# Sums of squares over partitions for nine RMS norms: ones as the weights in four column groups, in place of ones as the moving column

## The chip, the cores and the metric

The kernel runs on one core of one Trainium2 chip. The metric is the device time of one execution in microseconds (us); of several runs the median is given. The engines are named as in the profile: PE is TensorE's matmul, PEld its weight load, DVE is VectorE, ACT ScalarE, POOL GpSimd, SP the engine that issues most transfers.

## The reference

One layer of a decoder is applied to 1024 prompt tokens and 32 sample tokens, each a vector of 1024 numbers in float32. What matters here is how often a token's vector is normalized:

```python
def _rms(x, g):
    xf = x.astype(jnp.float32)
    y = xf * lax.rsqrt(jnp.mean(xf * xf, axis=-1, keepdims=True) + EPS)
    return (y * g.astype(jnp.float32)).astype(x.dtype)

def _layer(x, p, attn_fn, pool_prev, pos0, ...):
    h = _rms(x, n_mix_pre)
    z = h @ w_in                      # q, k, v and the pooling input
    ...                               # sliding-window attention, pooling mixer
    mix = jnp.concatenate([a, m], axis=-1) @ w_out
    x = x + _rms(mix, n_mix_post)
    f = _rms(x, n_ffn_pre)
    f = (jax.nn.silu(f @ w_gate) * (f @ w_up)) @ w_down
    x = x + _rms(f, n_ffn_post)
    x = x + jax.nn.sigmoid(x @ w_ple_gate) * (p @ w_ple)
    return x, k_state, v_state, pool_state
```

There are four norms per token. Each needs the sum of a token's 1024 squares, and then its reciprocal root as a factor for the whole vector.

## The kernel before

**Layout.** Features lie on the 128 partitions and tokens along the free dimension, so a vector of 1024 features is eight blocks of 128 partitions. The 1056 tokens form three groups, 0, 1 and 2, of 352 tokens each; group 2 holds the end of the prompt and the 32 sample tokens. Four norms for three groups are twelve norms. The three of the first kind come at the kernel's start, the other nine later.

**Matmuls.** Every operand is split into a high part (`wh`, `fh`, ...) that is rounded to a matmul type and the remainder (`wl`, `fl`, ...). A product of two operands is three matmuls: high by high, high by low, low by high (`gemm`). ScalarE makes the high part of a tile with a cast (L173), VectorE the low part with a subtraction (L174). Weights pass through four pairs of such tiles; a cast of new weights can start when TensorE is done with an older pair. A projection of one group onto 128 output features is 24 matmuls with 352 moving columns.

**One norm** is the generator `rstd_steps(acc)`. `acc` is a tile of 128 partitions by 352 tokens that holds partial sums of squares, so a sum over partitions is left to do. Three float32 matmuls take a block of 128 columns of `acc` as weights and one column of ones as what moves; each gives one column of a bank, with tokens on the partitions. ScalarE takes the root into `sd`, a tile of 128 by 3, VectorE its reciprocal, and splits it into a high and a low part (`hl`). Then two VectorE products spread each of the two parts on diagonals (`dg`), the generator pauses with a `yield`, and after it two matmuls with ones as weights turn the diagonals into a bank in which every partition holds the factors of all 352 tokens.

**What sets the order.** On TensorE the matmuls keep the order in which the program records them. Work that runs between projections is written as generators (`chain`). After every product the program calls `turn(n)` with the number of matmuls, which advances a clock, `now`; a generator whose due time has come is resumed there. A pause `yield load, wait` sets the next due time: the load divided by `share` is added to VectorE's planned clock and the wait to that. So the two numbers of a `yield` decide behind which matmuls the next matmul of that generator stands. On the other engines a scheduler sets the order when the program is built, and each engine then works strictly in it.

**Where the nine norms are.** `ffn_steps(g)` holds two for each group, `mix`'s norm and that ahead of the feed-forward part: between the two it scales and adds, squares, and sums (`sum_halves`). After the second it makes the gain products (L982, `y` from `x`, a gain column and the bank with the factors), four to each half of the features, and splits each half into `fh` and `fl`. Group 2's runs beside the last output projections, and its operand is read by the first feed-forward matmuls; those of groups 0 and 1 run beside the feed-forward matmuls of group 2. `x2_steps(g, operand)` holds the third norm of each group, behind the feed-forward part. The other names in the timelines: `mh`, `ml` are the mixed operands of the output projection, `acc<-acc,sq` (L854) adds a square to a sum of squares, `b` is a bank of PSUM.

Of the kernel before, what the change touches and what calls it, by code (L numbers as in the profile page):

```python
# [10 lines left out]
F32 = mybir.dt.float32  # L11
F32R = mybir.dt.float32r
AF = mybir.ActivationFunctionType
ALU = mybir.AluOpType
AX = mybir.AxisListType

P = 128
D = 1024
# [44 lines left out]
def trunk_kernel(  # L63
# [33 lines left out]
    te, ve, se, ge = nc.tensor, nc.vector, nc.scalar, nc.gpsimd  # L97
# [4 lines left out]
    spool = ctx.enter_context(tc.tile_pool(name="spool", bufs=2))  # L102
# [5 lines left out]
    def nm(s):  # L108
        cnt[0] += 1
        return f"{s}{cnt[0]}"  # L110

    def act_tile(shape, dt=F32, s="a"):
        return apool.tile(shape, dt, tag="a", bufs=A_SLOTS, name=nm(s))
# [12 lines left out]
    def mm(*args, **kw):  # L126

        ins = te.matmul(*args, **kw)  # L128
        if pinned[0]:
            tc.keep_in_program_order(ins)  # L130

    def bank():
        return psum.tile([P, 512], F32, tag="b", name=nm("b"))
# [4 lines left out]
    def const(shape, src=None, s="c", dt=F32):  # L138
        t = cpool.tile(shape, dt, name=nm(s))
        if src is not None:  # L140
            nc.scalar.dma_start(t, src)
        return t
# [3 lines left out]
    ident = const([P, P])  # L146
# [8 lines left out]
    ones = const([P, P])  # L155
    ge.memset(ones, 1.0)
    ones_r = const([P, P], dt=F32R)
    ge.tensor_copy(ones_r, ones)
    epst = const([P, 1])
# [7 lines left out]
    def fix(ins):  # L167

        if fixed[0]:
            tc.keep_in_program_order(ins)  # L170

    def split(hi, lo, src):
        fix(se.copy(hi, src))  # L173
        fix(ve.tensor_tensor(lo, src, hi.bitcast(F32), op=ALU.subtract))  # L174
# [177 lines left out]
            for k in range(KC)  # L352
        ]

    def rstd_steps(acc):

        n = acc.shape[1]
        sm = bank()  # L360
        for i in range(TB):
            at = min(i * P, n - P)
            mm(sm[:, i : i + 1], acc[:, at : at + P], ones[:, 0:1], start=True, stop=True)
        sd = spool.tile([P, TB], F32, tag="sd", name=nm("sd"))
        fix(se.activation(sd, sm[:, :TB], AF.Sqrt, bias=epst, scale=1.0 / D))
        fix(ve.reciprocal(sd, sd))
        hl = spool.tile([P, 2, TB], F32R, tag="hl", name=nm("hl"))
        fix(ve.tensor_copy(hl[:, 0], sd))
        fix(ve.tensor_tensor(hl[:, 1], sd, hl[:, 0].bitcast(F32), op=ALU.subtract))
        dgs = []  # L370
        dg2 = act_tile([P, 2, TB, P], F32R, "dg")
        for h in range(2):
            dg = dg2[:, h]
            fix(
                ve.tensor_tensor(
                    dg, diag, hl[:, h].bitcast(F32).unsqueeze(2).to_broadcast([P, TB, P]), op=ALU.mult
                )
            )
            dgs.append(dg.rearrange("p i k -> p (i k)"))
        yield 6, 14  # L380
        ps = bank()
        for h in range(2):
            mm(ps[:, :n], ones_r, dgs[h][:, :n], start=h == 0, stop=h == 1)
        return ps[:, :n]

    def acc_rows():
        t = act_tile([P, 4, NX], s="acc")
        return [t[:, g, : NS[g]] for g in range(G)]
# [30 lines left out]
    xs, acc1, r1 = [[None] * 2 for _ in range(G)], acc_rows(), [None] * G  # L419
# [105 lines left out]
    def u_prod(c, g, h):  # L525

        if h == 0:
            ups[c, g] = bank()
        ps = ups[c, g][:, : NS[g]]
        wh, wl = pairs[U0[c]]  # L530
        xh, xl = xs[g][h]
        for k in range(4):
            mm(ps, wh[:, 4 * h + k, :], xh[:, k, :], start=h == 0 and k == 0, stop=False)
            mm(ps, wh[:, 4 * h + k, :], xl[:, k, :], start=False, stop=False)
        for k in range(4):
            mm(ps, wl[:, 4 * h + k, :], xh[:, k, :], start=False, stop=h == 1 and k == 3)
# [5 lines left out]
    def u_norm(steps, g):  # L542
        try:
            next(steps)
        except StopIteration as e:
            fix(se.copy(acc1[g], e.value))
            r1[g] = acc1[g]

    pinned[0] = True
    norms = [None] * G  # L550
    norms[0] = rstd_steps(acc1[0])
    for h in range(2):
        for c in range(4):
            u_prod(c, 0, h)
# [11 lines left out]
    x_operand(2, 1)  # L566
    for c in range(4):
        u_prod(c, 1, 1)
    norms[1] = rstd_steps(acc1[1])
    u_norm(norms[1], 1)  # L570
    for h in range(2):
        u_prod(0, 2, h)
# [3 lines left out]
    for c in range(4):  # L576
        u_evict(c, 1)
        se.copy(u_decode(c)[:, :, 0:PST], stt[:, c])
    split(wplh, wpll, wpl)
    norms[2] = rstd_steps(acc1[2])  # L580
    u_norm(norms[2], 2)
    for h in range(2):
        u_prod(1, 2, h)
# [131 lines left out]
    def scores(b):  # L715


        t = act_tile([P, 8, WIN])
        nk = 2 * WIN if b else WIN
        lo = b * WIN + WIN - nk  # L720
        at = WIN * 4 // nk
        both = [[bank() for _ in range(4 // at)] for _ in range(2)]
        for c in range(4):
            for kv in range(2):
                rows = slice(64 * kv, 64 * kv + 64)
                i = c % at
                mm(
                    both[kv][c // at][:, i * nk : (i + 1) * nk],
                    qT[c][rows, b * WIN : (b + 1) * WIN],
                    kT[rows, lo : lo + nk],  # L730
                    start=True,
                    stop=True,
                )
        for kv in range(2):
            tk = t[:, 4 * kv : 4 * kv + 4, :]
            for i, ps in enumerate(both[kv]):
                tc_ = tk[:, i * at : (i + 1) * at, :]
                v = ps.rearrange("p (c k) -> p c k", k=nk)
                if b:
                    m = am[:, 0, :].unsqueeze(1).to_broadcast([P, at, WIN])  # L740
                    se.copy(tc_, v[:, :, :WIN])
                    ve.copy_predicated(tc_, m.bitcast(mybir.dt.int32), v[:, :, WIN:])
                else:
                    ve.tensor_tensor(tc_, v, m4(1), op=ALU.add)
            hs = slice(4 * kv, 4 * kv + 4)
            softmax(tk, 4, 0.125, skp[:, hs], nskp[:, hs])
        return t
# [98 lines left out]
    acc = acc_rows()  # L846
# [46 lines left out]
    t = scores(order[0])  # L893
# [16 lines left out]
    for a, b in zip(order, order[1:] + [None]):  # L910
# [11 lines left out]
        t = t2  # L922
# [559 lines left out]
```

## Time and profile before

| What | us |
|---|---|
| median of 3 runs (1087.38 to 1088.51) | 1088.09 |
| the profiled execution's own time | 1088.29 |
| its span, first to last instruction | 1086.5 |
| PE busy in the span | 1076.8 |
| PEld busy | 1060.1 |
| DVE busy | 873.2 |
| ACT busy | 512.4 |
| POOL busy | 283.2 |

A row of a timeline gives the start and the length in us, the engine, the line, the operation, what is written and what is read, the shapes and the number of instructions that the row merges; in brackets stand the idle time of the engine ahead of it and what ended that. For a matmul what moves is named first and the weights second: in `b<-fh,wh` the operand moves and the weights are loaded. Ends of matmuls are modelled and overlap, so the starts are what tells TensorE's pace. A float32 matmul appears as two instructions. A row of a stage table gives the stage, its length, and for PE, PEld, DVE, ACT and POOL the busy time with the number of instructions in brackets, then the clock that was granted to TensorE, the busy share of the DMA engines and GB/s. A row of the chain of waits gives a start, a length, and the engine and line that the end was waiting for in that time. A row of a group of instructions ends with the busy time, the mean ns of one, and the engine's idle time ahead of them.

### The profile page before, as it was taken

How to read it: one execution, taken by the hardware profiler on the slowest of the kernel's cores; microseconds unless marked ns; L12 is line 12 of the kernel's file. 1: busy time of each engine (PE TensorE's matmuls, PEld its weight loads, DVE VectorE, ACT ScalarE, POOL GpSimd, SP SyncE). 2: the span in 40 equal slices, each digit the busy share in tenths (PEclk: the TensorE clock that was granted, in tenths of full speed). 3: DMA queues.
4: the chain of work that ended last, by engine and by line, in shares of the span. 5: the costliest groups of instructions: out<-in, count | busy, mean ns of one | idle time of the engine just before them, and what ended most of it. 6: DMA issues, size and time to landing. Idle time of an engine off the chain costs nothing.

```text
span 1086.5 us, 17727 instructions
## 1 busy us (share of the span) xinstructions
PE 1076.8 (99%) x6867; PEld 1060.1 (98%) x6867; DVE 873.2 (80%) x1312; ACT 512.4 (47%) x877; POOL 283.2 (26%) x212
## 2 busy tenths in 40 slices
PE   9999999999999999999999999999999999999998
PEld 8999988899999999999999999999998999999998
DVE  6777478886878956796598898898899997969973
ACT  7423277774555533345543343443344365545531
POOL 0073032200000023436545445454442000022300
PEclk9999999999999999999999999999999999999999
DMA  8121311534553432322222222212234556553461
GB/s 296 59 72 39 120 50 40 188 143 141 190 184 130 136 117 78 131 78 78 78 79 78 83 74 85 91 59 97 79 112 161 170 179 224 182 210 125 135 203 60
DMA packets 43572, 131.27 MB, mean 121 GB/s; under 512 B 5060, under 2 KB 15588, under 8 KB 43488
## 3 DMA queue, kind: packets, MB, share of 16 engines
q1 hardware_dynamic: 42160, 128.38, 34.7%
q10 hardware_dynamic: 1328, 1.77, 0.5%
q8 instruction: 54, 0.88, 0.3%
q14 instruction: 30, 0.25, 0.1%
HBM read 114.25 MB, written 15.87 MB: 120 GB/s over the span
## 4 chain that ended last, share of the span: by engine, by line
PE 95%; DVE 3%; POOL 1%; ACT 1%; issue 1%; DMA 0%; SPq 0%; DVEq 0%; POOLq 0%; ACTq 0%
PE b L128 94%; PE b L122 1%; POOL wr L1058 1%; DVE sl L174 1%; DMA xr<-in_x_dram 0%; DVE hp L174 0%; DVE a L805 0%; DVE ap L1228 0%; ACT a L701 0%; DVE wl L174 0%; DVE hf L1133 0%; POOL a L707 0%; DVE w L174 0%; ACT sh L173 0%; DVE fl L174 0%
## 5 line engine op out<-in xcount | busy, mean ns | idle before, releaser
L1058 POOL TENSOR_TENSOR wr<-wr,wr 128x512 f32<-128x512 f32 x108 | 174.0, 1625 | 482.2 <-DMA wr<-in_w_gu_dram 242.3
L173 ACT CAST wh<-wr 128x1024 fp32r<-128x1024 f32 (+1 forms) x138 | 142.1, 1031 | 164.3 <-PE b L128 92.2
L174 DVE TENSOR_TENSOR wl<-wr,wh 128x1024 fp32r<-128x1024 f32 (+1 forms) x138 | 168.1, 1219 | 51.4 <-ACT wh L173 35.4
L128 PE MATMUL b<-fh,wh 128*128 128x352 f32 x624 | 201.5, 323 | 0.0
L128 PE MATMUL b<-fh,wl 128*128 128x352 f32 x624 | 200.0, 320 | 0.0
L128 PE MATMUL b<-fl,wh 128*128 128x352 f32 x624 | 199.9, 320 | 0.0
L173 ACT CAST sh<-wr 128x1024 fp32r<-128x1024 f32 x72 | 75.7, 1051 | 138.0 <-POOL wr L1058 131.9
L128 PE MATMUL b<-fh,sh 128*128 128x352 f32 x416 | 134.3, 323 | 0.0
L128 PE MATMUL b<-fl,sh 128*128 128x352 f32 x416 | 133.2, 320 | 0.0
L128 PE MATMUL b<-fh,sl 128*128 128x352 f32 x416 | 133.2, 320 | 0.0
L174 DVE TENSOR_TENSOR sl<-wr,sh 128x1024 fp32r<-128x1024 f32 x72 | 97.5, 1356 | 36.1 <-ACT sh L173 18.2
L128 PEld LDWEIGHTS b<-fl,wh 128*128 128x128 f32 x624 | 117.4, 188 | 0.0
L128 PEld LDWEIGHTS b<-fh,wh 128*128 128x128 f32 x624 | 117.0, 188 | 0.0
L128 PEld LDWEIGHTS b<-fh,wl 128*128 128x128 f32 x624 | 116.9, 187 | 0.0
L128 PE MATMUL b<-h,wh 128*128 128x352 f32 x480 | 105.6, 326 | 0.6 <-ACT h L426 0.6
L128 PE MATMUL b<-hid,wh 128*128 128x352 f32 x416 | 99.6, 322 | 0.0
L128 PEld LDWEIGHTS b<-h,wh 128*128 128x128 f32 x480 | 82.4, 190 | 1.6 <-ACT h L426 0.9
L1058 POOL TENSOR_TENSOR wr<-wr 128x512 f32<-128x512 f32 x36 | 51.0, 1416 | 105.9 <-DVE w L174 105.9
L128 PEld LDWEIGHTS b<-fl,sh 128*128 128x128 f32 x416 | 78.2, 188 | 0.0
L128 PEld LDWEIGHTS b<-fh,sh 128*128 128x128 f32 x416 | 78.0, 188 | 0.0
L128 PEld LDWEIGHTS b<-fh,sl 128*128 128x128 f32 x416 | 77.9, 187 | 0.0
L128 PE MATMUL b<-hp,sh 128*128 128x352 f32 x320 | 76.7, 322 | 0.8 <-DVE p L1085 0.6
(195 smaller groups left out, 2245.7 us busy)
## 6 DMA issues: line engine op xcount, KB each, us to landing
wr<-in_w_gu_dram SPq DMA_DIRECT2D x88, 512.0 KB, 3.3
wr<-in_w_dn_dram SPq DMA_DIRECT2D x40, 512.0 KB, 3.2
wr<-in_w_pg_dram SPq DMA_DIRECT2D x16, 512.0 KB, 3.5
x<-in_x_dram SPq DMA_DIRECT2D x6, 704.0 KB, 9.9
x1d<-x SPq DMA_DIRECT2D x6, 704.0 KB, 3.6
x<-x1d SPq DMA_DIRECT2D x6, 704.0 KB, 5.7
out_y_dram<-yo SPq DMA_DIRECT2D x24, 176.0 KB, 1.9
wr<-in_w_out_b_dram SPq DMA_DIRECT2D x8, 512.0 KB, 3.3
```

The lines of the kernel that those rows point to most:

```text
L122: ins = te.transpose(out, src, ident)
L128: ins = te.matmul(*args, **kw)
L173: fix(se.copy(hi, src))
L174: fix(ve.tensor_tensor(lo, src, hi.bitcast(F32), op=ALU.subtract))
L1058: ge.tensor_tensor(out, a, b, op=op)
```

## The change

The old generator is kept under the name `rstd_first` for the three norms at the start. A new `rstd_steps` serves the other nine:

- The ones become the weights, 32 columns of them, and `acc` moves: four float32 matmuls of 88 columns each, the j-th written to partitions 32j to 32j + 31 of one bank. Each group of 32 partitions then holds, on every partition, the sums of one quarter of the tokens.
- Root, reciprocal and split are done on 128 by 88 in place of 128 by 3. The high and low part live in the tile `dg` itself, in its last two slices.
- In place of the diagonals two VectorE products, of 352 columns and not 384, take every 32nd column of the identity, which keeps the partitions 0, 32, 64 and 96, one for each quarter.
- The two spreading matmuls are as before.
- The pause is `yield 8, 22` in place of `yield 6, 14`.

```diff
-    def rstd_steps(acc):
+    def rstd_first(acc):
...
+    def rstd_steps(acc):
+        w = acc.shape[1] // 4
+        sm = bank()
+        for j in range(4):
+            mm(sm[32 * j : 32 * j + 32, :w], ones[:, :32], acc[:, j * w : (j + 1) * w], start=True, stop=True)
+        t = act_tile([P, 10, w], F32R, "dg")
+        sd, hl = spool.tile([P, w], F32, tag="sw", name=nm("sw")), t[:, 8:10]
+        se.activation(sd, sm[:, :w], AF.Sqrt, bias=epst, scale=1.0 / D)
+        ve.reciprocal(sd, sd)
+        ve.tensor_copy(hl[:, 0], sd)
+        ve.tensor_tensor(hl[:, 1], sd, hl[:, 0].bitcast(F32), op=ALU.subtract)
+        lead = ident[:, ::32].unsqueeze(2).to_broadcast([P, 4, w])
+        for h in range(2):
+            part = hl[:, h].bitcast(F32).unsqueeze(1).to_broadcast([P, 4, w])
+            ve.tensor_tensor(t[:, 4 * h : 4 * h + 4], lead, part, op=ALU.mult)
+        yield 8, 22
+        ps = bank()
+        for h in range(2):
+            mm(ps[:, : 4 * w], ones_r, t[:, 4 * h : 4 * h + 4].rearrange("p i k -> p (i k)"), start=h == 0, stop=h == 1)
+        return ps[:, : 4 * w]
...
-    norms[0] = rstd_steps(acc1[0])
+    norms[0] = rstd_first(acc1[0])
```

The same one-word edit is made for `norms[1]` and `norms[2]`.

The pause moves six of the nine pairs of spreading matmuls to a later place, by 12, 24 or 36 matmuls. The one that the prediction follows is the second norm of group 2. On TensorE, before (bank `b_2861` gets the factors; `b_2869` is the next output projection):

```order
L128 MATMUL b_2823<-mh_734,wh_2591 128x352
L128 MATMUL b_2823<-ml_735,wh_2591 128x352
L128 MATMUL b_2823<-mh_734,wl_2592 128x352
L128 MATMUL b_2861<-dg_2820,c_89 128x352 x2
L128 MATMUL b_2869<-mh_1861,wh_2672 128x352
L128 MATMUL b_2869<-ml_1862,wh_2672 128x352
L128 MATMUL b_2869<-mh_1861,wl_2673 128x352
```

And after the change, where that output projection is called `b_2861` and the factors' bank `b_2896`:

```order
L128 MATMUL b_2861<-mh_734,wh_2672 128x352
L128 MATMUL b_2861<-ml_735,wh_2672 128x352
L128 MATMUL b_2861<-mh_734,wl_2673 128x352
L128 MATMUL b_2896<-dg_2815,c_89 128x352 x2
L128 MATMUL b_2904<-mh_1861,wh_2678 128x352
L128 MATMUL b_2904<-ml_1862,wh_2678 128x352
L128 MATMUL b_2904<-mh_1861,wl_2679 128x352
```

The 24 matmuls of one output projection, which stood behind the two spreading matmuls, now stand ahead of them.

On VectorE the same place, before: from the second weight split behind the factors on (`y_1287` and `y_1960` are the two halves of group 2's operand, `fl_2905` and `fl_2985` their low parts, `b_2861` the factors):

```order
L174 TENSOR_TENSOR wl_2899<-wr_2857,wh_2898 128x1024
L854 TENSOR_TENSOR acc_1301<-acc_1301,sq_2895 128x352
L982 SCALAR_TENSOR_TENSOR y_1960<-x_2486,c_72,b_2861 128x352
L174 TENSOR_TENSOR fl_2905<-y_1287,fh_2904 128x1408
L982 SCALAR_TENSOR_TENSOR y_1960<-x_2486,c_72,b_2861 128x352
L174 TENSOR_TENSOR wl_2938<-wr_2859,wh_2937 128x1024
L854 TENSOR_TENSOR acc_1301<-acc_1301,sq_2934 128x352
L174 TENSOR_TENSOR fl_2985<-y_1960,fh_2984 128x1408
L174 TENSOR_TENSOR wl_2979<-wr_2902,wh_2978 128x1024
```

And after the change, from the same weight split, that of `wr_2857`, on; their line, L982, is L1006 there, and L854 is L878 (the factors are in `b_2896`, the low parts are `fl_2940` and `fl_2985`):

```order
L174 TENSOR_TENSOR wl_2891<-wr_2857,wh_2890 128x1024
L878 TENSOR_TENSOR acc_1301<-acc_1301,sq_2887 128x352
L1006 SCALAR_TENSOR_TENSOR y_1287<-x_2484,c_72,b_2896 128x352 x2
L1006 SCALAR_TENSOR_TENSOR y_1960<-x_2486,c_72,b_2896 128x352 x2
L174 TENSOR_TENSOR wl_2934<-wr_2859,wh_2933 128x1024
L878 TENSOR_TENSOR acc_1301<-acc_1301,sq_2930 128x352
L1006 SCALAR_TENSOR_TENSOR y_1960<-x_2486,c_72,b_2896 128x352
L174 TENSOR_TENSOR fl_2940<-y_1287,fh_2939 128x1408
L1006 SCALAR_TENSOR_TENSOR y_1960<-x_2486,c_72,b_2896 128x352
L174 TENSOR_TENSOR wl_2973<-wr_2894,wh_2972 128x1024
L878 TENSOR_TENSOR acc_1301<-acc_1301,sq_2969 128x352
L174 TENSOR_TENSOR fl_2985<-y_1960,fh_2984 128x1408
```

Each low part stands one weight split (`wl`) further back than before: the first behind the split from `wr_2859`, the second behind the one after it.

More of the change, by code (lines that the diff above doesn't have):

```diff
@@ L568, in trunk_kernel @@
         u_prod(c, 1, 1)
-    norms[1] = rstd_steps(acc1[1])
+    norms[1] = rstd_first(acc1[1])
     u_norm(norms[1], 1)
@@ L579, in trunk_kernel @@
     split(wplh, wpll, wpl)
-    norms[2] = rstd_steps(acc1[2])
+    norms[2] = rstd_first(acc1[2])
     u_norm(norms[2], 2)
```

## The prediction

> **What bounds the kernel now.** I read the page's busy shares first, then TensorE's busy time by stage, then the chain of waits, and last the timelines at the places that the change touches.
>
> ```profile
> PE 1076.8 (99%) x6867; PEld 1060.1 (98%) x6867; DVE 873.2 (80%) x1312; ACT 512.4 (47%) x877; POOL 283.2 (26%) x212
> 210.00:290.00 80.00, 80.00 (x523) 77.72 (x522) 60.55 (x97) 46.12 (x84) 2.21 (x2) 1.00 0.47 163
> 290.00:420.00 130.00, 130.00 (x823) 130.00 (x822) 101.18 (x126) 64.78 (x83) 12.77 (x8) 1.00 0.42 142
> 216.86 570.56 PE b L128 x3604
> 830.30 252.08 PE b L128 x1584
> ```
>
> The first number after a stage's length is TensorE's busy time. In the two stages that hold the first six of the nine norms it is the whole stage: TensorE never waits there. The chain of waits says the same: two unbroken stretches of matmuls, 570.56 and 252.08 us long, hold all nine. So a nanosecond of TensorE's sequence is a nanosecond of the kernel, while work on VectorE or ScalarE costs nothing until it makes TensorE wait. The clock column is 1.00, so no gate enters.
>
> **The sums themselves.** A float32 matmul appears as two passes. One norm of before, the pair of norms of groups 0 and 1, and the nearest work that already uses column groups, the attention's value products:
>
> ```profile
> 253.74 0.32 PE L128 MATMUL b<-mh,wl 128*128 128x352 f32 x1
> 253.90 0.72 PE L128 MATMUL b<-c,acc 128*128 128x1 f32 x6
> 254.49 0.41 PE L128 MATMUL b<-mh,wh 128*128 128x352 f32 x1
> 254.73 0.33 PE L128 MATMUL b<-ml,wh 128*128 128x352 f32 x1
> 273.86 0.32 PE L128 MATMUL b<-fh,wl 128*128 128x352 f32 x1
> 274.02 1.39 PE L128 MATMUL b<-c,acc 128*128 128x1 f32 x12
> 275.52 0.32 PE L128 MATMUL b<-fl,wh 128*128 128x352 f32 x1
> 211.95 0.32 PE L128 MATMUL b<-mh,wl 128*128 128x352 f32 x1
> 212.21 1.68 PE L128 MATMUL b<-a,a 128*64 128x256 f32 x16
> 214.08 0.32 PE L128 MATMUL b<-ml,wh 128*128 128x352 f32 x1
> L128 PE MATMUL b<-a,a 64*128 64x256 f32 x112 | 14.0, 389 | 0.0
> L128 PE MATMUL b<-a,a 64*128 64x512 f32 x8 | 2.0, 615 | 0.0
> ```
>
> A projection matmul starts every 0.16 us. From 253.74 to 254.73 are 0.99 us where two such steps would be 0.32: one norm's sums cost 0.67. From 273.86 the pair costs 1.66 - 0.32 = 1.34. Seven single norms and one pair: 7 x 0.67 + 1.34 = 6.0 us, removed.
>
> What takes their place is eight passes of 88 columns. The value products bound it: (214.08 - 211.95) - 0.32 = 1.81 us for 16 passes of 256 columns. A column costs (615 - 389) / 256 = 0.88 ns, a pass 0.23; one behind another they would take 3.6 us, so they overlap. In the code eight go two at a time in two column groups and eight four at a time in quadrants: six waves, 1.36 us. The other 0.45 is for entering this form, passing between its two kinds and leaving it (the first step in, 0.26 in place of 0.16, shows part of it). Of these three changes a norm has the two outer ones, and I charge 0.35 to them. A new norm is then two waves of 88 x 0.88 ns = 0.08 and 0.35: 0.51, a gain of 0.16; the pair shares one entry, 0.35 + 4 x 0.08 = 0.67 or a little more, say 0.70, a gain of 0.64. Sum: 7 x 0.16 + 0.64 = **-1.8 us**.
>
> No row shows four groups of 32 with 128 rows each, so this is bounded on both sides. Without any cost to enter, only two waves and the long step after them (0.24 for 0.16) are left, 0.24 a norm and 0.40 the pair: -4.0 us. If the groups took turns, eight passes at 0.08 to 0.10 (0.59 / 6 of the old ones) with the 0.35 make 0.97 to 1.15 a norm and 1.6 to 1.95 the pair: +2.3 to +4.0. I take -1.8, since two and four tiles at once are what the nearest rows show.
>
> The Trainium skill's "TensorE: Matmul & The Clock Gate", section "LDWEIGHTS (loading the stationary operand)", lets a load take its columns over 1.2 GHz: 107 ns for 128, near the 98 of the old passes. By it eight loads of 32 columns are 8 x 27 = 0.21 us; if they queue, a norm is 0.57 and the gain 7 x 0.10 + 0.5 = 1.2 us, the sum below 0.6 higher.
>
> **What moves.** The spreading matmuls stay two per norm, but the new numbers at the pause put them later: for the second norm of token group 2 a whole projection of 24 matmuls later. Behind them stand the gain products (L982), the casts into fh and the subtractions into fl, and the first feed-forward matmuls read those at a fixed place of TensorE's order.
>
> ```profile
> 258.44 0.48 PE L128 MATMUL b<-dg,c 128*128 128x352 f32 x2
> 270.21 0.32 PE L128 MATMUL b<-fh,wh 128*128 128x352 f32 x1
> 270.37 0.32 PE L128 MATMUL b<-fl,wh 128*128 128x352 f32 x1
> 272.27 0.32 PE L128 MATMUL b<-fl,wh 128*128 128x352 f32 x1
> 258.97 1.07 DVE L982 SCALAR_TENSOR_TENSOR y<-x,c,b 128x352 f32<-128x352 f32 x2 [1.98 <-PE b L128]
> 265.84 1.63 DVE L174 TENSOR_TENSOR fl<-y,fh 128x1408 fp32r<-128x1408 f32 x1
> 267.88 1.22 DVE L174 TENSOR_TENSOR wl<-wr,wh 128x1024 fp32r<-128x1024 f32 x1
> 269.01 0.52 DVE L854 TENSOR_TENSOR acc<-acc,sq 128x352 f32<-128x352 f32 x1
> 269.63 1.62 DVE L174 TENSOR_TENSOR fl<-y,fh 128x1408 fp32r<-128x1408 f32 x1
> 262.62 1.05 ACT L173 CAST wh<-wr 128x1024 fp32r<-128x1024 f32 x1 [2.28 <-PE b L128]
> 266.48 1.05 ACT L173 CAST wh<-wr 128x1024 fp32r<-128x1024 f32 x1 [0.74 <-ACT fh L173]
> 268.23 1.37 ACT L173 CAST fh<-y 128x1408 fp32r<-128x1408 f32 x1
> 270.29 1.05 ACT L173 CAST wh<-wr 128x1024 fp32r<-128x1024 f32 x1 [0.69 <-ACT fh L173]
> 271.25 0.55 ACT L873 ACTIVATE y<-b,c 128x352 f32<-128x352 f32 x1
> 271.70 0.45 ACT L853 ACTIVATE sq<-b 128x352 f32<-128x352 f32 x1
> ```
>
> Before, the halves of fl end at 267.47 and 271.25 and are first read at 270.37 and 272.27: 2.9 and 1.0 us to spare. I walk VectorE's new order with these durations, on before's clock; the sums' gain up to there shifts all engines alike. The spreading matmul comes 24 x 0.16 = 3.8 us later, 262.26; VectorE's first product 0.53 after it, as before, 262.79. An instruction holds its engine for its duration less the 0.09 by which the next one starts early (267.88 + 1.22 against 269.01): two products 0.98, a weight's low part 1.13, a sum of squares 0.43, fl 1.54.
> - Two products to 263.77; wl (its cast ended at 263.67) to 264.9; acc to 265.35; four products to 267.3.
> - wl, whose cast ends at 267.53 and follows TensorE's pace, 267.55 to 268.7; acc to 269.15; a product to 269.63; only now fl's first half (ScalarE now casts its fh in the slot of 268.23): it ends at 271.25. TensorE reads it at 270.37: **0.9 us** of waiting.
> - The last product from 271.17 to 271.66; wl (cast from 270.29 to 271.34) to 272.8; acc to 273.24. ScalarE's next fh follows that cast, a scaling and a square, which as before end at 272.15, so it starts at 272.05 and ends at 273.42. fl's second half: 273.45 to 275.07.
> - TensorE, 0.9 late, wants this fh (one matmul ahead of fl's 272.27) at 273.0 and has it at 273.45, wants fl at 273.6 and has it at 275.1. In all it reads that row at 275.1 in place of 272.27: **+2.8 us**, bounds 2.5 and 3.1 by 0.3 of slips in the walk.
>
> Queued behind those matmuls are all later ones, in one unbroken chain, so nothing gives it back: the waits near 820 belong to work that TensorE itself paces, and shift with it.
>
> **What costs nothing, and its cover.** The other late spreads move 12 to 36 matmuls, 1.9 to 5.7 us, and feed operands with more to spare. The operand of groups 0 and 1 that is nearest to its reader is the first pair of rows here, the last norm of group 2 the second:
>
> ```profile
> 380.11 1.63 DVE L174 TENSOR_TENSOR fl<-y,fh 128x1408 fp32r<-128x1408 f32 x1 [0.40 <-ACT fh L173]
> 400.36 0.32 PE L128 MATMUL b<-fl,w 128*128 128x352 f32 x1
> 1027.71 1.63 DVE L174 TENSOR_TENSOR fl<-x,fh 128x1408 fp32r<-128x1408 f32 x1
> 1046.13 0.32 PE L128 MATMUL b<-fl,wh 128*128 128x352 f32 x1
> 882.84 1.02 DVE L375 TENSOR_TENSOR dg<-c,hl 128x384 fp32r<-128x384 f32 x2
> 885.34 0.48 PE L128 MATMUL b<-dg,c 128*128 128x352 f32 x2
> L705 DVE RECIPROCAL sm<-sm 128x4 f32<-128x4 f32 x16 | 2.8, 173 | 0.3
> L705 DVE RECIPROCAL sm<-sm 128x1 f32<-128x1 f32 x2 | 0.3, 154 | 0.2 <-DVE sm L704 0.2
> ```
>
> 18.6 and 16.8 us are there; two delayed spreads of one operand take at most 11. VectorE's small steps now have 88 columns instead of 3. The reciprocal is between 1 ns a column (as its plain operations of 352 columns in 0.52 us) and (173 - 154) / 3 = 6 ns: +0.1 to +0.5 us; cast and subtraction +0.1 each, the two products 32 columns shorter, -0.07; the square root about +0.05. So 0.3 to 0.7 us a norm. The tightest unmoved spread, at 885.34, had its tile at 883.86: 1.5 us. Without that cover it would cost at most 0.7 a norm.
>
> **Sum.** -1.8 + 2.8 = +1.0 us on the profiled execution's 1088.29 (span 1086.5, 1.8 around it): 1089.3. The median shown, 1088.09, is 0.2 below it: **1089.1**.
>
> **Rivals.**
> - *The groups take turns*, in all nine sums. For it: no row with four groups of 32. Against: the value products' overlap. It decides once a pass waits for its neighbour's 0.08 us. +2.8 + 3.2 = +6.0: 1094.1, slower.
> - *Entering and leaving eats the gain.* The ends cost 0.51 instead of 0.35 a norm, all of the 0.45 and more. For it: the block is 0.16 us of work inside 0.35 of switching. Against: part of the 0.45 lies between the two kinds of tiles. +2.8: 1090.9, slower.
> - *The operand is not late*, the stall hidden as the other spreads' are. For it: VectorE sat idle 1.98 us before 258.97 and can work ahead. Against: the walk has put the work of that gap first already, and two of its waits follow TensorE. -1.8, with cheap switching -4.0: 1086.3 to 1084.1, faster only past the first.
>
> **How the numbers follow.** A measurement of this kernel tells about 0.2%, 2.2 us, from no change: outside 1085.9 to 1090.3. The forecast has 0.63, its own range 1088.0 to 1090.3 (2.5 - 2.6 to 3.1 - 0.9); of it 0.59 is same, 0.03 slower, 0.01 faster. Turns 0.11, slower. Eaten gain 0.12, 0.11 of it slower. No stall 0.14, 0.09 faster, 0.05 same. That makes faster 0.10, same 0.65, slower 0.25. The range leaves out the turns and the part of the last rival past -1.8: 1086.3 to 1091.2.
>
> **What would show it.** In the changed profile: eight passes b<-acc,c within 0.3 us of their first, and the step past them 0.45 to 0.6 us longer than two projection steps; if starts lie 0.08 apart each, the turns. In the chain of waits a break of TensorE near 270 to 275 ending on fl L174 and fh L173, 2.5 to 3.1 us in all; without it the walk was wrong. No break elsewhere that before lacks; one at 885 would mean the reciprocal. The spread of the last norm and TensorE's busy time in 290 to 420 should read as before.

## The result

| | time, median (runs) | ratio to before, 95% interval | profiled execution's span |
|---|---|---|---|
| before | 1088.3 us (1087.4 to 1088.8) | | 1086.5 us |
| changed | 1094.4 us (1093.7 to 1095.6) | 1.0053 (1.0039 to 1.0068) | 1092.2 us |

The changed kernel is 6 us slower. The forecast was 1089.1 us, with a range up to 1091.2. The measured time is nearly that of the rival in which the groups take turns, 1094.1, but the profile shows that its mechanism is not what happened.

**The new sums** are as cheap as forecast. TensorE's timeline of the changed kernel (start, duration in us), a single norm and the pair of groups 0 and 1:

```profile
254.26 0.32 PE L128 MATMUL b<-mh,wl 128*128 128x352 f32 x1
254.51 0.36 PE L128 MATMUL b<-acc,c 128*32 128x88 f32 x8
254.80 0.43 PE L128 MATMUL b<-mh,wh 128*128 128x352 f32 x1
255.07 0.32 PE L128 MATMUL b<-ml,wh 128*128 128x352 f32 x1
...
277.14 0.32 PE L128 MATMUL b<-fh,wl 128*128 128x352 f32 x1
277.40 0.51 PE L128 MATMUL b<-acc,c 128*32 128x88 f32 x16
277.84 0.43 PE L128 MATMUL b<-fh,wh 128*128 128x352 f32 x1
278.10 0.32 PE L128 MATMUL b<-fl,wh 128*128 128x352 f32 x1
```

From 254.26 to 255.07 are 0.81 us, less two steps 0.49; the pair takes 0.96 - 0.32 = 0.64. Eight passes lie within 0.29 us, and eight more add 0.15: they overlap. The single records say how: four passes start within 0.02 us, the other four 0.10 us behind them and again within 0.02. These are the two waves that the forecast counted at 0.08 us each.

**The wait** is there too, at the rows forecast:

```profile
270.54 0.32 PE L128 MATMUL b<-fh,wh 128*128 128x352 f32 x1
271.64 0.43 PE L128 MATMUL b<-fl,wh 128*128 128x352 f32 x1 [0.77 <-DVE fl L174]
273.36 0.32 PE L128 MATMUL b<-fh,wl 128*128 128x352 f32 x1
273.79 0.42 PE L128 MATMUL b<-fh,wh 128*128 128x352 f32 x1
275.45 0.43 PE L128 MATMUL b<-fl,wh 128*128 128x352 f32 x1 [1.24 <-DVE fl L174]
```

Against a step of 0.16 the three breaks cost 0.94, 0.27 and 1.50 us, 2.7 in all; 0.9, 0.45 and 1.5 were forecast. Behind the first and the last break one more step is 0.1 us longer than usual, so the wait is 2.9 us in all.

**What was missed** lies in no gap. The view of busy time by stage (length, TensorE's busy time and its matmuls, granted clock, share and rate of the transfers), for the same 470 us of the feed-forward part in both kernels, first before, then changed:

```profile
345.00:815.00 470.00, 470.00 (x2960) 1.00 0.27 91
```

```profile
345.00:815.00 470.00, 470.00 (x2940) 1.00 0.27 92
```

TensorE is busy throughout at full granted clock in both, and does 20 matmuls fewer. From the matmul that follows the last spread to the one ahead of the next break, in the timelines of before and of the changed kernel:

```profile
337.27 0.48 PE L128 MATMUL b<-hid,wh 128*128 128x352 f32 x2
...
818.55 0.32 PE L128 MATMUL b<-hp,sl 128*128 128x352 f32 x1
```

```profile
345.36 0.32 PE L128 MATMUL b<-fh,wh 128*128 128x352 f32 x1
...
824.24 0.32 PE L128 MATMUL b<-hp,sl 128*128 128x352 f32 x1
```

The start times of the records in nanoseconds give, as means, 158.89 ns for one step (from one matmul's start to the next) in the first, over 3029 steps, and 160.00 in the second, over 2993. In each of these stretches the steps repeat with a period of six, to a nanosecond, whichever tiles are multiplied. Worked out from the records, the mean of each of the six (the third row is from before, 840 to 875 us):

```
six steps, ns                                sum      three steps
161.7  155.8  160.8  155.0  159.2  160.8     953.3    476.7
157.4  161.6  159.2  160.8  161.9  159.1     960.0    480.0
164.4  159.0  158.3  159.3  164.0  161.7     966.7    483.3
```

In the records TensorE's stream runs in one of three patterns, keeps it for up to 480 us, and leaves it only at an odd operation: a spread (the two spreading matmuls of a norm), a norm's sums, a wait. Below, a pattern is named by its time for three steps, and it is read from the one profiled execution of each kernel. In before every spread is followed by 476.7 ns, and six of the eight places with old sums by 483.3. In the changed kernel every spread is followed by 480.0 and all new sums by 476.7.

**The ledger** of the two profiled executions, 1092.2 - 1086.5 = 5.7 us, from equal matmuls' start times: +0.6 ahead of the first of the nine norms, where nothing was changed; sums -1.95 (7 x 0.18 + 0.70); the wait +2.9; a shorter one at 890, +0.35; breaks near 820, which vary, -0.3; and what is left, +4.1, is the pattern. By count: some 4,600 steps at +1.11 ns are 5.1, less some 460 steps that before spent in the slowest pattern, at 2.2 ns, 1.0: +4.1 as well.

### The profile page after: what moved, and what is told of

It reads as the page before. It is cut to its first block, busy times and chain, and to the rows that moved or that the text cites. A ratio compares the mean times of both kernels' runs of the same rounds, so it can differ in the third digit from the quotient of the medians.

```text
span 1092.2 us, 17760 instructions
## 1 busy us (share of the span) xinstructions
PE 1080.7 (99%) x6885; PEld 1059.9 (97%) x6885; DVE 876.7 (80%) x1312; ACT 512.9 (47%) x877; POOL 283.6 (26%) x212
## 4 chain that ended last, share of the span: by engine, by line
PE 71%; DVE 2%; POOL 1%; issue 0%; ACT 0%; DVEq 0%; POOLq 0%
PE b L128 71%; POOL wr L1082 1%; DVE sl L174 1%; DVE fl L174 0%; DVE ap L1252 0%; DVE wl L174 0%; DVE hf L1157 0%; DVE w L174 0%; DVE hp L174 0%; ACT sh L173 0%; DVE c L1191 0%; ACT fh L173 0%; DVE p L1109 0%; DVE c L1109 0%; DVE u L1109 0%
```

## The experiments

Each ratio is to the kernel before on the same chip. Where only the pattern is in question, the stage of 345 to 815 us tells it: 2960 matmuls for 476.7 ns, 2939 or 2940 for 480.0. All starts of an operand are counted in bytes from the start of its tile; where the tiles themselves start is not looked at.

**Are place, sums or tile behind the pattern?** Four kernels. The first is the changed kernel with the old pause:

```diff
-        yield 8, 22
+        yield 6, 14
```

> The changed kernel with its new sums and the old pause, so that every spread stands where it stood before. All theories: the 2.9 us of waiting for fl and fh between 270 and 276 go, and the sums keep their gain of 2.0 us. What is in dispute is the rest of the loss, 4 us that lie in no gap: in the changed profile three steps of TensorE take 480.0 ns behind every spread, where before they took 476.7. Theory LAYOUT (the new spread reads its second half 1408 bytes behind the first instead of 1536, and that leaves the slower pattern) and theory SUMS (the new sums leave it to whatever follows): the slower pattern stays, 1091.3 us. Theory PLACE (the later place of the spread sets it): the slower pattern goes, 1086.7 us.

Measured: 1090.5 us, ratio 1.0014 (1.0005 to 1.0024). By stages:

```profile
210.00:290.00 80.00, 80.00 (x535) 1.00 0.49 167
345.00:815.00 470.00, 470.00 (x2939) 1.00 0.27 91
```

The wait near 270 is gone (80.00 of 80 us busy), the slower pattern is not. PLACE falls. Not every stretch shows 480.0, though: behind the pair of spreads of groups 0 and 1, which here follow each other at once, the records show 476.7 ns (252 steps, 0.3 us less), and behind two spreads that waited for their tiles 483.3 (647 steps, 0.7 us more). The time is 0.8 us under the forecast; these stretches don't explain that, and the kernel's own runs lie further apart (1089.5 to 1091.7).

The second is the kernel before with the new pause for the nine norms:

```diff
-        yield 6, 14
+        yield (6, 14) if first else (8, 22)
```

> The kernel before with only the new pause, for the nine norms: old sums, spreads late. All theories: waits for fl and fh of 2.8 us in all near 270, as in the changed kernel. LAYOUT and SUMS: three steps behind a spread stay at 476.7 ns, 1091.1 us. PLACE: they take 480.0 ns, 1095.3 us.

Measured: 1091.8 us, ratio 1.0029 (1.0017 to 1.0041). Timeline and stage of this kernel:

```profile
271.77 0.43 PE L128 MATMUL b<-fl,wh 128*128 128x352 f32 x1 [0.81 <-DVE fl L174]
...
275.54 0.43 PE L128 MATMUL b<-fl,wh 128*128 128x352 f32 x1 [1.23 <-DVE fl L174]
```

```profile
345.00:815.00 470.00, 470.00 (x2960) 1.00 0.28 92
```

The same waits with the old sums, and the faster pattern: the later place costs some 3 us through the operand alone, as the forecast's walk through VectorE's queue had it.

The third leaves the changed kernel as it is, but for where the halves of the spread's moving tile lie; `TB * P` is 384 columns, 1536 bytes:

```diff
-        t = act_tile([P, 10, w], F32R, "dg")
-        sd, hl = spool.tile([P, w], F32, tag="sw", name=nm("sw")), t[:, 8:10]
+        raw = act_tile([P, 2 * TB * P + 2 * w], F32R, "dg")
+        hl = raw[:, 2 * TB * P :].rearrange("p (h k) -> p h k", k=w)
+        halves = [raw[:, h * TB * P : h * TB * P + 4 * w] for h in range(2)]
+        sd = spool.tile([P, w], F32, tag="sw", name=nm("sw"))
...
-            ve.tensor_tensor(t[:, 4 * h : 4 * h + 4], lead, part, op=ALU.mult)
+            ve.tensor_tensor(halves[h].rearrange("p (i k) -> p i k", k=w), lead, part, op=ALU.mult)
...
-            mm(ps[:, : 4 * w], ones_r, t[:, 4 * h : 4 * h + 4].rearrange("p i k -> p (i k)"), ...)
+            mm(ps[:, : 4 * w], ones_r, halves[h], ...)
```

> The changed kernel, but the two halves of the spread's moving tile lie 1536 bytes apart as before, instead of 1408; sums, pause and all orders as in the changed kernel. LAYOUT: three steps behind every spread take 476.7 ns again; about 4650 steps by 1.1 ns are 5.2 us less, 1089.2 us. SUMS and PLACE: 480.0 ns stay, 1094.4 us.

Measured: 1089.7 us, ratio 1.0011 (1.0000 to 1.0022).

```profile
345.00:815.00 470.00, 470.00 (x2960) 1.00 0.27 91
```

The fourth does the reverse to the kernel before, in the nine norms:

```diff
-        dg2 = act_tile([P, 2, TB, P], F32R, "dg")
+        far = TB * P if first else n
+        dg2 = act_tile([P, far + TB * P], F32R, "dg")
...
-            dg = dg2[:, h]
+            dg = dg2[:, h * far : h * far + TB * P].rearrange("p (i k) -> p i k", k=P)
```

> The kernel before, but in the nine norms the two halves of the spread's moving tile lie 1408 bytes apart instead of 1536 (the second product overwrites the 32 unused columns of the first); sums, pause and all orders as before. LAYOUT: three steps behind every spread take 480.0 ns, some 4650 steps by 1.1 ns: 1093.5 us. SUMS and PLACE: 476.7 ns stay, 1088.3 us.

Measured: 1093.8 us, ratio 1.0044 (1.0029 to 1.0059).

```profile
345.00:815.00 470.00, 470.00 (x2939) 1.00 0.28 92
```

Both times came out as LAYOUT has it, to 0.5 us. In the third all nine spreads are followed by 476.7 ns. In the fourth all are followed by 480.0 but the first, which waited 1.2 us, and the pair of groups 0 and 1; there the records show 476.7. With orders, sums and pause untouched, 128 bytes in the start of one operand are worth some 5 us either way (1094.4 to 1089.7, 1088.6 to 1093.8). SUMS falls with the fourth, which has the old ones.

**One spread is enough, and it remembers.** From here on a spread is called aligned when its second half starts at 1536 bytes (12 times 128) and misaligned when it starts at 1408 (11 times 128). Only the last spread ahead of the long stretch is made misaligned, in the kernel before:

```diff
+        far = n if near else TB * P
...
-        r = yield from rstd_steps(acc[g])
+        r = yield from rstd_steps(acc[g], g == 1)
```

> The kernel before, but in a single spread of the nine, the last of group 1 at 337 us, the second half starts at 1408 bytes instead of 1536. Theory: a spread sets the pattern of all that follows until the next odd operation. From 337 to 818 us some 3030 steps at 480.0 instead of 476.7 ns for three: 3.4 us more, 1091.8 us, and 476.7 ns behind all other spreads. Rival: the slower pattern needs many such spreads, or belongs to the tile's place in memory, and one does nothing: 1088.4 us.

Measured: 1091.5 us, ratio 1.0032 (1.0020 to 1.0045).

```profile
345.00:815.00 470.00, 470.00 (x2939) 1.00 0.27 91
```

One matmul's start address costs 3.2 us. Behind the other spreads the records show 476.7 ns. The reverse, that one spread aligned in the changed kernel, the eight others not:

> The reverse: the changed kernel, but in that one spread, at 345 us there, the second half starts at 1536 bytes. Theory: from 345 to 824 us three steps take 476.7 ns, 3.3 us less: 1091.1 us, with 480.0 ns behind all other spreads. Rival: one aligned spread doesn't bring a stream back that an earlier one has slowed: 1094.4 us.

Measured: 1094.2 us, ratio 1.0053 (1.0038 to 1.0068).

```profile
345.00:815.00 470.00, 470.00 (x2939) 1.00 0.27 91
```

A miss: the rival holds. The spread of group 0, 6 us earlier and misaligned, had set 480.0, and the aligned one left it so. So both were aligned (`g != 2` in place of `g == 1`):

> The changed kernel with both of the last spreads ahead of the long stretch, groups 0 and 1 at 339 and 345 us, at aligned starts; the other spreads as in the changed kernel. Theory, amended after the run with one aligned spread: an aligned spread keeps the pattern that it meets, a misaligned one turns 476.7 into 480.0 ns. The sums at 326 and 333 leave 476.7, so it holds from 333 to 824 us: 3000 steps by 1.1 ns are 3.3 us less than the changed kernel, 1091.1 us. Rival: with the new sums, it takes all nine spreads aligned, or the pattern of the earlier stretches returns: 480.0 ns, 1094.3 us.

Measured: 1090.8 us, ratio 1.0019 (1.0010 to 1.0029).

```profile
345.00:815.00 470.00, 470.00 (x2960) 1.00 0.27 92
```

The amended theory holds here: an aligned spread that meets 476.7 ns leaves it, a misaligned one between the same matmuls turns it into 480.0. (An aligned one that meets 483.3, behind the old sums, is followed by 476.7.) Behind misaligned pairs and behind misaligned spreads that waited, the first and the fourth kernel above have shown other patterns too.

**What is misaligned?** The kernel with new sums, old pause and halves at 0 and 1536 bytes is the base here; it has a paragraph of its own below. The edit is the pair of starts, in columns of 4 bytes; the tile is made longer to hold the halves:

```diff
-        halves = [raw[:, h * TB * P : h * TB * P + 4 * w] for h in range(2)]
+        halves = [raw[:, at : at + 4 * w] for at in (0, 416)]
```

The two other kernels have (32, 384) and (32, 416).

> As the kernel with new sums, old pause and far halves, but the second half starts 1664 bytes behind the start of the tile (13 times 128) instead of 1536 (12 times 128). Theory ALIGNMENT (a half that starts at an odd multiple of 128 bytes, as 1408 is, leaves the slower pattern): 480.0 or more ns behind the spreads, 1089 to 1091 us. Theory TOUCHING (two halves without a gap between them leave it): 476.7 ns, 1086 us.

> The same with halves at 128 and 1536 bytes: they touch, 1408 apart, and it is the first half that starts at an odd multiple of 128. TOUCHING: the slower pattern, 1089 to 1091 us. ALIGNMENT: the slower pattern too if any half counts, 476.7 ns and 1086 us if only the last one does.

> The same with halves at 128 and 1664 bytes: 1536 apart as in the kernel before, with a gap, but both at odd multiples of 128. ALIGNMENT: the slower pattern, 1089 to 1091 us. TOUCHING, or the distance alone: 476.7 ns, 1086 us.

Measured: 1090.6 us, ratio 1.0021 (1.0011 to 1.0031); 1088.0, 0.9997 (0.9987 to 1.0007); 1093.8, 1.0050 (1.0031 to 1.0068). The stages in that order:

```profile
345.00:815.00 470.00, 470.00 (x2939) 1.00 0.27 91
```

```profile
345.00:815.00 470.00, 470.00 (x2960) 1.00 0.28 92
```

```profile
345.00:815.00 470.00, 470.00 (x2939) 1.00 0.27 92
```

TOUCHING falls with the first and the third, whose halves have a gap; the third has the old distance of 1536 too, so it isn't the distance either. The third shows 480.0 and 483.3 and no 476.7 behind any spread. Its time, of two runs alone, lies 2.8 us above what was expected; the 483.3 ns behind three of its spreads and behind the pair, 1349 steps by 1.1 ns, are 1.5 us of that. The second is mixed and lies between what was expected: 476.7 in the long stretch, but 483.3 ns behind three of its spreads. So a start at an odd multiple of 128 bytes can disturb in either half; which pattern follows also depends on what stands around it. Starts that are no multiple of 128 were not tried.

**Is the pattern of the stream itself made by such starts?** Four slices of a moving operand start at 0, 1408, 2816 and 4224 bytes, so at even, odd, even, odd multiples of 128, for three matmuls each: a period of six. The kernel before, with them taken in another order:

```diff
+        if last % 4 == 3:
+            ops = [ops[k + j] for k in range(0, len(ops), 4) for j in (0, 2, 1, 3)]
```

> The kernel before with one change in the order of the products inside a sum: where four slices of an operand are summed (they start 0, 1408, 2816 and 4224 bytes into the tile, so at even, odd, even, odd multiples of 128), they are taken 0, 2, 1, 3; spreads, sums and pause as before. Before, the repeating pattern is six steps long, 953.3 ns, as long as one even and one odd slice of three matmuls each. Theory CHANGE (each change between even and odd start costs time, and the pattern is made by them): the pattern becomes twelve steps long with half as many changes. A spread with one half at an odd start has two more changes and took 483 instead of 477 ns, so a change is worth some 3 ns; half of two changes per six steps is 0.5 ns a step, some 3 us in all: 1085.6 us. Theory SPREAD ONLY (the start of a slice has no part in the pattern of the stream): six steps and 953.3 ns stay, 1088.5 us.

Measured: 1091.3 us, ratio 1.0027 (1.0017 to 1.0038).

```profile
345.00:815.00 470.00, 470.00 (x2946) 1.00 0.27 91
```

Both theories miss. The six-step pattern is gone, so SPREAD ONLY falls: the order of the slices has a part in it. But the mean rose to 159.6 ns, with a looser repeat every 36 steps, where CHANGE promised less, so the number of changes between even and odd is not the price. Whether it is the moving slices' starts is not shown: the slices of the weights are taken in the new order too. What inside TensorE keeps such a pattern is left open.

**A better kernel.** New sums, old pause, aligned halves:

> The three findings put together: new sums, old pause, halves 1536 bytes apart. Sums 2.0 us less than before, no wait for fl near 270, 476.7 ns for three steps behind every spread, and behind the sums too, where before some 480 steps took 161.1 ns each (1.1 us). Theory LAYOUT: 1088.6 - 2.0 - 0.5 to 1.1 = 1085.5 to 1086.1 us, faster than both kernels. If the pattern behind a spread hangs on the new sums or on chance instead, some stretches read 480.0 or 483.3 ns and the time lies between 1087 and 1090.5 us.

Measured: 1087.0 us, ratio 0.9986 (0.9977 to 0.9995), 476.7 ns behind every spread, but 1 us over the forecast. The profiled execution is the slowest of its eleven (1085.0 to 1088.4); it was 2.3 us late before the first of the nine norms. TensorE's and VectorE's timelines of this kernel:

```profile
885.54 0.86 PE L128 MATMUL b<-dg,c 128*128 128x352 f32 x2 [0.76 <-DVE dg L405]
```

```profile
883.82 0.70 DVE L399 RECIPROCAL sw<-sw 128x88 f32<-128x88 f32 x1
884.56 0.21 DVE L400 CAST dg<-sw 128x88 fp32r<-128x88 f32 x1
884.80 0.25 DVE L401 TENSOR_TENSOR dg<-sw,dg 128x88 fp32r<-128x88 f32 x1
884.96 0.95 DVE L405 TENSOR_TENSOR dg<-c,dg 128x352 fp32r<-128x352 f32 x2
```

The spread takes 1.3 us longer here than where nothing is late: its tile is ready at 885.9. How long it waits in the faster executions is not known. So the last three norms got a longer pause:

```diff
-        yield 6, 14
+        yield (20, 14) if late else (6, 14)
```

> The kernel with new sums, old pause and far halves, but for the last three norms the pause is longer, so that their spreads stand 24, 12 and 24 rows later. There the spread at 885 had waited 1.3 us for the second half of its tile, since the new small steps on VectorE take 0.6 us longer. Theory: that wait goes, the gain of the sums shows, 1.3 us less than that kernel's 1087.0: 1085.7 us. Rival: the operand behind the later spread is late in its turn, or the sum of VectorE's work decides there, and the wait only moves: 1087.0 us.

Measured: 1085.7 us, ratio 0.9974 (0.9966 to 0.9983).

```profile
886.72 0.48 PE L128 MATMUL b<-dg,c 128*128 128x352 f32 x2
```

The two spreading matmuls take 0.48 us again, as in before, and the wait has not come up elsewhere. This kernel beats before by 2.6 us, clear of the noise. The 1.3 us to the kernel without the longer pause are as forecast, but the two intervals overlap a little, so that step is probable and not shown.

## Why the prediction was wrong

- **Sums: right.** Forecast -1.8 us, measured -1.95; 0.51 and 0.70 us for a norm and the pair against 0.49 and 0.64. The rival of groups that take turns falls by the rows at 254.51 and 277.40, although its time fits. By an estimate from the page of the Trainium skill "TensorE: Matmul & The Clock Gate", section "LDWEIGHTS (loading the stationary operand)", eight loads of 32 columns take 0.21 us if they queue; eight more passes added only 0.15 here, so in this trace they don't queue at that price.
- **The late operand: right.** 2.8 us forecast, 2.9 measured, in the three places; with the old sums it came alone, and it went with the old pause.
- **VectorE's small steps: the size right, the cover not.** The columns are busy time and the mean in ns; first the changed kernel, then before:

```profile
L397 DVE RECIPROCAL sw<-sw 128x88 f32<-128x88 f32 x9 | 6.1, 692 | 0.5 <-ACT sw L396 0.5
L399 DVE TENSOR_TENSOR dg<-sw,dg 128x88 fp32r<-128x88 f32 x9 | 2.2, 249 | 0.2
L398 DVE CAST dg<-sw 128x88 fp32r<-128x88 f32 x9 | 2.0, 227 | 0.2
```

```profile
L366 DVE RECIPROCAL sd<-sd 128x3 f32<-128x3 f32 x12 | 1.9, 169 | 2.6 <-ACT sd L365 2.6
L368 DVE CAST hl<-sd 128x3 fp32r<-128x3 f32 x12 | 2.2, 189 | 0.3
L369 DVE TENSOR_TENSOR hl<-sd,hl 128x3 fp32r<-128x3 f32 x12 | 1.9, 161 | 0.3
```

  The reciprocal costs (692 - 169) / 85 = 6.2 ns a column, just past the upper bound of 6; a norm's steps grow by 0.6 us, inside 0.3 to 0.7. But of the 1.5 us to spare at 885 nothing was left: VectorE came to that reciprocal 6.3 us behind the sums instead of 5.4, and TensorE waited 0.35 us. The forecast had set one tile's slack against one norm's growth, as if VectorE's queue ahead of it stood still. It doesn't: VectorE came 7.2 us behind the sums, and TensorE waited 1.3, with old pause and aligned halves; it was 5.9 us behind, without a wait, with old pause and misaligned ones. Even with the old sums and misaligned halves it was 6.5, and there the shorter steps left no wait. What moves the queue stays open.
- **The step that failed** is "The spreading matmuls stay two per norm": their cost was put at nothing but their place. Their tile had moved from halves 1536 bytes apart to 1408, and the argument took a matmul step for the constant 0.16 us that the timeline prints. At the new start the spreads left each step behind them 1.1 ns longer, and that term measures +4.1 us, nearly all of the 4.7 us between the forecast's +1.0 and the profiled +5.7. The rest is the 0.6 us at the start and the wait of 0.35 at 890, less some 0.35 of small terms. The profile of before would have warned. Two stages of 30 us, both wholly busy:

```profile
842.00:872.00 30.00, 30.00 (x188) 1.00 0.54 186
930.00:960.00 30.00, 30.00 (x191) 1.00 0.52 186
```

  With equal clock and equal shapes of the matmuls, the first holds three fewer. That a step isn't constant stood there, and "a nanosecond of TensorE's sequence is a nanosecond of the kernel" holds for it too.
- **The rivals.** Eaten gain and hidden operand both fall by the rows above. None of them, nor the range, allowed for a change in TensorE's rate while it is busy. That the measured time lies 0.3 us from the rival with the turns is chance.

## What to carry to other kernels

Where TensorE is busy throughout, count the matmuls in stages of equal length before and after: a share of 99% and a full clock don't tell that each step has become 0.7% longer. When a tile that a few odd matmuls read is laid out anew, keep its starts at the multiples that they had (here even multiples of 128 bytes), or measure the new ones; in these runs an operand's start was worth more than the gain of the sums. And walk every operand with little slack through the other engine's queue, including those whose place does not move.

## What was not expected of the hardware

- A long stream of equal matmuls, 352 columns each with its own weights, ran at a mean of 158.9, 160.0 or 161.1 ns a step, in exact six-step patterns. What chose among them were single operations up to 480 us earlier. One start address changed by 128 bytes cost 3.2 us (1091.5 against 1088.3).
- The Trainium skill's "SBUF — State Buffer", section "Operand start alignment", asks that an operand start at a multiple of its element size and says that its runs timed nothing. The starts tried here, multiples of 128 bytes for elements of 4, obey that; the runs show that among such starts the time still differs (1094.4 against 1089.7 us).
- In every run the new sums leave the fastest pattern, where some of the old ones leave 161.1 ns. In before some 200 steps stand behind such sums, about 0.45 us, a gain of the new sums that no row of single instructions shows. Before's other 255 steps at 161.1 ns stand behind breaks near 820 and 839 us; what follows those differs from kernel to kernel with the same sums.
- In the changed order of slices the stream took 159.6 ns with a loose repeat every 36 steps. Why the slices in their own order are the faster of the two tried, and what carries the pattern, stays open.
